# Attention pieces written between contraction steps, transposes two tiles behind scores, and the query-key products in one block

## The chip, the cores and the metric

One core of a Trainium2 chip. Its engines are TensorE (PE), VectorE (DVE), ScalarE (ACT), GpSimd (POOL) and SyncE (SP, which here issues most DMAs). The metric is the device time of one launch, in microseconds.

## What is computed

A decoder trunk of two layers over 512 tokens of width 1024. Layer 0 mixes tokens with a gated DeltaNet (6 heads of width 128), layer 1 with attention over a sliding window of 128 (12 heads of width 64, one sink logit per head). In both layers four heads also attend to 256 fixed memory tokens. Each layer ends in an output projection and a SwiGLU block. Cut to what the change touches:

```python
# layer 0: what the DeltaNet needs of its queries
qkv = silu(causal_depthwise_conv(proj, conv_w))            # q, k, v of six heads
intra = einsum("bhncd,bhnkd->bhnck", q, k) * decay          # query-key products
sol = triangular_solve(lower, rhs, unit_diagonal=True)      # then a scan over chunks
# both layers
def memory_attention(q, mem_k, mem_v):
    s = einsum("bshd,bmhd->bhsm", q, mem_k) * MEM_DH ** -0.5
    return einsum("bhsm,bmhd->bshd", softmax(s), mem_v)
# layer 1, per head; s is masked to the window
m = max(max(s), sink);  p = exp(s - m)
o = (p / (sum(p) + exp(sink - m))) @ v
x = x + concat([mix, mem_o]) @ w_out
```

## The kernel before

Activations lie transposed: eight tiles (k = 0 to 7) of 128 features by 512 tokens. A product with a weight (`project`) is a sum of eight contraction steps into one PSUM bank, and each step (`mm3`) is three matmuls of 128x512: high part of the weight by high and by low part of the activation, and low part of the weight by high part of the activation. The weight's high part `whi` is an ACT copy, its low part `wlo` a DVE subtraction; `split` makes an activation's pair `h`, `l` in the same way (copy L148, subtraction L161).

The code is written in program order, and a scheduler takes that order as priority when it places each engine's instructions. Each engine then works off its own queue in order, and semaphores hold an instruction until its inputs and its buffers are there. Named pools give the buffers; PSUM banks too come from pools (layer 0: three `pj`, two `g`, three `sc`; layer 1's attention: two `pj`, two `pt`, one each of `g`, `qk`, `sc`).

Attention for a tile of two heads is in four parts. `scores` makes the products of queries and keys (in `qk`, or in `g` and `sc` in layer 0) for the four blocks of 128 queries, and in layer 1 the masked row maxima (`sm`, `stats`). `soften` takes exponents and scales them by the reciprocal sums, half of the blocks on ACT (L148), half on DVE (L168). `weigh` transposes the probabilities on PE (L158, into `pt` or `g`), copies them out of PSUM (`pf`), multiplies with the values (into `sc`) and splits the result (`h`, `l`).

In layer 0 (`gdn`) the order is: scores of memory head pair 0, the inverse of the 32x32 diagonal blocks (`base_inverse`), query 0, transposes and sums of pair 0, query 1, scores of pair 1, query 2, transposes and sums of pair 1, and then a loop over the six heads, in which queries 3 to 5 are computed, each query tile gets its silu (ACT), and its product with the normalized keys `kn` goes to PE (bank `g`) and on to DVE. A query is a `project` and a depthwise convolution: one ACT copy with a scale and three DVE taps (`conv_tile`). The values' projection and the solve come next. The exponents need one table of ACT's functions, the silus another (`use`).

In layer 1 (`swa`) tiles 0 to 5 are window heads, 6 and 7 memory heads. For tile t the loop writes: the projection of the queries of tile t+1, scores of t, transposes and sums of t-1, the softmax of t. `output` then runs eight projections with w_out, one after the other.

Of the kernel before, what the change touches and what calls it, by code (L numbers as in the profile page):

```python
# [18 lines left out]
P = 128  # L19
T = 512  # L20
# [68 lines left out]
class Builder:  # L89
# [152 lines left out]
    def build(self):  # L242
        tc, nc, a = self.tc, self.nc, self.a
        with ExitStack() as st:
# [23 lines left out]
            with self.banks(pj=2, g=1, qk=1, pt=2, sc=1):  # L268
                with opened("swa", side="right") as sp:
                    mix = self.swa(sp)  # L270
                h = self.output(xp, 1, mix, self.apool)
# [185 lines left out]
    def normed(self, m):  # L457

        return self.project(self.a["win"][m], self.h)

    def conv_tile(self, m, out):

        ps = self.normed(m)
        tap = lambda j: self.gains[:, G_CONV + 4 * m + j:G_CONV + 4 * m + j + 1]
        self.copy(out, ps, scale=tap(3))
        for j in (2, 1, 0):
            s = 3 - j
            self.stt(out[:, s:], ps[:, :T - s], tap(j), out[:, s:], ALU.mult, ALU.add)
        return out

    def gdn(self, gp):
# [86 lines left out]
        query = lambda h: self.conv_tile(h, self.t(gp, [P, T], F32, "qv", 5))  # L558

        def remember(m):  # L560
            got = self.scores(gp, qm[m], self.memK[m], False)
            self.soften(gp, got, None)
            return got

        self.use(LN_EXP)
        got = remember(0)
        X, Tt = self.base_inverse(gp, base_in)
        for i in range(NH):
            h, c = divmod(i, NC)
            self.copy(kg[h][:, c, :], kg[h][:, c, :], scale=f[:, 2, i:i + 1])  # L570
        ts = [query(0)]
        self.weigh(gp, got, self.memV, 0, mq[0], False)
        ts.append(query(1))
        got = remember(1)
        ts.append(query(2))
        self.weigh(gp, got, self.memV, 1, mq[1], False)
        self.use(SILU_SIN)
        for h in range(H):
            if h + 3 < H:
                ts.append(query(h + 3))  # L580
            t = ts[h]
            self.fn(t, t, AF.Silu)
            ps = self.bank("g")
# [7 lines left out]
            nc.sync.dma_start(q2[h], sq)  # L591
        AT = DT
# [156 lines left out]
    def scores(self, pool, q, kk, win):  # L749

        nc = self.nc
        own = "pt" in self.pbufs
        half = [slice(0, 64), slice(64, P)]
        sm = [self.t(pool, [P, 2, 2, 2 * P], F32, "sm", 6 if own else 2) for _ in range(2)]
        sm = [t[:, n] for t in sm for n in range(2)]
        stats = self.t(pool, [P, 4, 2 * NC], F32, "stats", 3 if own else 2)
        mx, den, nm, es = (stats[:, i, :] for i in range(4))
        for n0 in range(0, NC, 2):
# [5 lines left out]
            for n in (n0, n0 + 1):  # L764
                ks = slice((n - 1) * P if n else 0, (n + 1) * P) if win else slice(0, ML)
                c0 = P if win and n == 0 else 0
                for b in range(2):
                    self.scored = self.mm(ps[b][:, n - n0, c0:], q[half[b], n * P:(n + 1) * P], kk[half[b], ks])
# [15 lines left out]
        return sm, mx, den, nm, es  # L784

    def soften(self, pool, scores, sinks):

        nc = self.nc
        win = sinks is not None
        sm, mx, den, nm, es = scores  # L790
        if win:
            sk = sinks.unsqueeze(2).to_broadcast([P, 2, NC])
            v4 = lambda ap: ap.rearrange("p (b n) -> p b n", b=2)
            self.stt(v4(mx), v4(mx), 0.125, sk, ALU.mult, ALU.max)
            self.ts(nm, mx, -1.0, ALU.mult)
            self.tt(nc.vector, v4(es), v4(nm), sk, ALU.add)
            self.fn(es, es, AF.Exp)
            for n in range(NC):
                c0 = 0 if n else P
                for b in range(2):  # L800
                    i = b * NC + n
                    self.fn(sm[n][:, b, c0:], sm[n][:, b, c0:], AF.Exp, scale=0.125, bias=nm[:, i:i + 1],
                            accum_out=den[:, i:i + 1])
            self.tt(nc.vector, den, den, es, ALU.add)
        nc.vector.reciprocal(den, den)
        for n in range(NC):
            k0 = 1 if win and n == 0 else 0
            p = sm[n][:, :, k0 * P:]
            dn = den.rearrange("p (b n) -> p n b", b=2)[:, n, :]
            for b in range(2):  # L810
                if n % 2:
                    self.copy(p[:, b], p[:, b], scale=dn[:, b:b + 1])
                else:
                    self.ts(p[:, b], p[:, b], dn[:, b:b + 1], ALU.mult)

    def weigh(self, pool, scores, vv, m, out, win):

        nc = self.nc
        own = "pt" in self.pbufs
        half = [slice(0, 64), slice(64, P)]  # L820
        sm = scores[0]
        o = self.bank("sc")
        group = NC if own else 2
        for n in range(NC):
            if n % group == 0:
                pf = {}
            k0 = 1 if win and n == 0 else 0
            pt = self.bank("pt" if own else "g", [P, 2, 2, P])
            for j in range(k0, 2):
                for b in range(2):  # L830
                    turned = self.tr(pt[:, j, b, :], sm[n][:, b, j * P:(j + 1) * P])
                    if own and self.scored is not None:

                        self.nosync(turned, self.scored)
                        self.scored = None
            pf[n] = self.t(pool, [P, 2, 2, P], F32, "pf", group)
            if own and n == 2:
                nc.vector.tensor_copy(pf[n][:, k0:], pt[:, k0:])
            else:
                self.copy(pf[n][:, k0:], pt[:, k0:])  # L840
            if (n + 1) % group:
                continue
            for n, t in pf.items():
                for j in range(1 if win and n == 0 else 0, 2):
                    for b in range(2):
                        v = vv[n - 1 + j][:, half[b]] if win else vv[j][:, m * P + 64 * b:m * P + 64 * b + 64]
                        ins = self.mm(o[half[b], n * P:(n + 1) * P], v, t[:, j, b, :], win and n == 0 or j == 0, j == 1)
                        if turned is not None:
                            self.nosync(ins, turned)
                            turned = None  # L850
        self.split(o, *out)


    def output(self, xp, layer, mix, hpool):
# [5 lines left out]
        for m in range(KD):  # L860
            ps = self.project(a["wout"][layer, m], mix, ("pj", "pj", "g")[m % 3],
                              (6, 7, 0, 1, 2, 3, 4, 5))
# [4 lines left out]
            self.acc = self.accumulate(xp, self.acc, self.x[m])  # L867
        return h
# [237 lines left out]
    def swa(self, sp):  # L1106
# [10 lines left out]
        def queries(t):  # L1117
            ps = self.project(a["wq"][t], h)
# [7 lines left out]
            else:  # L1126
                self.tt(nc.vector, qs[t], ps, self.rstd, ALU.mult)

        def keys():
            kk.append(self.t(sp, [P, T], F32, "ks"))  # L1130
            self.rope(sp, self.project(a["wkv"][0], hk), kk[0])

        def values():
            ps = self.project(a["wkv"][1], hk)
# [13 lines left out]
        def score(t):  # L1148
            got[t] = self.scores(sp, qs[t], kk[0] if t < 6 else memK[t - 6], t < 6)

        def soften(t):
            self.soften(sp, got[t], sinks[:, t, :] if t < 6 else None)

        def weigh(t):
            mix[t] = self.pair(self.bpool)
            if t < 6:
                self.weigh(sp, got[t], vv, t, mix[t], True)
            else:
                self.weigh(sp, got[t], memV, t - 6, mix[t], False)

        got = {}
        queries(6)
        queries(7)
        keys()
        values()
        score(6)
        soften(6)
        transpose_values()
        queries(0)
        score(7)  # L1170
        weigh(6)
        soften(7)
        last = 7
        for t in range(6):
            if t < 5:
                queries(t + 1)
            score(t)
            weigh(last)
            soften(t)
            last = t  # L1180
        weigh(last)
        return [mix[t] for t in range(KD)]
# [88 lines left out]
```

## Time and profile before

| What | Value |
|---|---|
| median of three runs | 1155.75 us |
| the three runs | 1155.51, 1155.75, 1159.62 us |
| the profiled execution | 1153.46 us, its span 1151.7 us |
| granted TensorE clock | 0.998 |
| PE busy | 1129.2 us, 98% of the span |
| DVE busy | 842.4 us, 73% |
| ACT busy | 632.1 us, 55% |
| POOL busy | 86.1 us, 7% |

A row of the timeline gives the start, the duration, the engine, the source line, the operation, what it writes and reads, the tile's shape, and how many instructions the row stands for; in brackets the engine's idle time before it and what ended that. Names lose their buffer numbers there. Start times are counted from the span's beginning.

### The profile page before, as it was taken

How to read it: one execution, taken by the hardware profiler on the slowest of the kernel's cores; microseconds unless marked ns; L12 is line 12 of the kernel's file. 1: busy time of each engine (PE TensorE's matmuls, PEld its weight loads, DVE VectorE, ACT ScalarE, POOL GpSimd, SP SyncE). 2: the span in 40 equal slices, each digit the busy share in tenths (PEclk: the TensorE clock that was granted, in tenths of full speed). 3: DMA queues.
4: the chain of work that ended last, by engine and by line, in shares of the span. 5: the costliest groups of instructions: out<-in, count | busy, mean ns of one | idle time of the engine just before them, and what ended most of it. 6: DMA issues, size and time to landing. Idle time of an engine off the chain costs nothing.

```text
span 1151.7 us, 19665 instructions
## 1 busy us (share of the span) xinstructions
PE 1129.2 (98%) x7476; PEld 990.3 (86%) x7476; DVE 842.4 (73%) x1587; ACT 632.1 (55%) x1271; POOL 86.1 (7%) x97
## 2 busy tenths in 40 slices
PE   7999999999999999999999999999999999999996
PEld 6888778887889998899998777778899988999986
DVE  5764877767789987389876767859799843898754
ACT  7579563366566652256654547675566622566533
POOL 0220000000111100011100000010011100111000
PEclk9999999999999999999999999999999999999999
DMA  8333342235557754567723421144478743577232
GB/s 310 118 121 110 120 101 95 85 106 162 167 138 186 191 126 127 160 147 187 181 69 103 134 79 38 40 110 129 115 186 193 180 112 103 147 190 184 70 95 93
DMA packets 73971, 152.83 MB, mean 133 GB/s; under 512 B 17756, under 2 KB 18420, under 8 KB 73876
## 3 DMA queue, kind: packets, MB, share of 16 engines
q1 hardware_dynamic: 62356, 130.59, 36.5%
q0 software_dynamic: 11520, 20.98, 11.6%
q8 instruction: 59, 0.97, 0.4%
q14 instruction: 36, 0.29, 0.1%
HBM read 144.58 MB, written 6.96 MB: 132 GB/s over the span
## 4 chain that ended last, share of the span: by engine, by line
PE 89%; DVE 6%; ACT 3%; DMA 1%; issue 1%; SPq 0%; DVEq 0%; ACTq 0%
PE pj L154 43%; PE g L154 38%; PE sc L154 5%; DVE wlo L161 2%; ACT sm L142 1%; PE pt L158 1%; PE qk L154 1%; ACT whi L148 1%; PE g L158 1%; DMA wraw<-in_wmk 1%; DVE stats L778 1%; DVE l L164 0%; DMA wraw<-in_win 0%; DVE x L164 0%; DVE btmp L161 0%
## 5 line engine op out<-in xcount | busy, mean ns | idle before, releaser
L148 ACT ACTIVATE whi<-wraw 128x512 fp32r<-128x512 f32 (+2 forms) x331 | 244.1, 746 | 253.6 <-PE pj L154 156.3
L161 DVE TENSOR_TENSOR wlo<-wraw,whi 128x512 fp32r<-128x512 f32 (+2 forms) x331 | 274.5, 839 | 104.7 <-ACT whi L148 98.4
L154 PE MATMUL pj<-h,whi 128*128 128x512 f32 (+1 forms) x676 | 266.4, 396 | 0.0
L154 PE MATMUL pj<-l,whi 128*128 128x512 f32 (+1 forms) x676 | 264.7, 392 | 0.4 <-DVE l L164 0.4
L154 PE MATMUL pj<-h,wlo 128*128 128x512 f32 (+1 forms) x676 | 264.0, 391 | 0.0
L154 PE MATMUL g<-T,whi 128*128 128x256 f32 x1280 | 228.1, 278 | 0.2
L154 PEld LDWEIGHTS g<-T,whi 128*128 128x128 f32 x1280 | 194.7, 188 | 1.8 <-DVE fu L164 1.8
L154 PE MATMUL g<-T,wlo 128*128 128x256 f32 x640 | 177.8, 278 | 0.0
L154 PEld LDWEIGHTS pj<-h,whi 128*128 128x128 f32 x676 | 126.8, 188 | 29.4 <-issue 3.6
L154 PEld LDWEIGHTS pj<-l,whi 128*128 128x128 f32 x676 | 127.1, 188 | 27.3 <-issue 1.8
L154 PEld LDWEIGHTS pj<-h,wlo 128*128 128x128 f32 x676 | 127.0, 188 | 25.7 <-issue 0.8
L154 PE MATMUL g<-l,whi 128*128 128x256 f32 (+1 forms) x508 | 144.4, 284 | 0.0
L154 PE MATMUL g<-h,whi 128*128 128x256 f32 (+1 forms) x508 | 144.3, 284 | 0.0
L154 PE MATMUL g<-h,wlo 128*128 128x256 f32 (+1 forms) x508 | 144.3, 284 | 0.0
L154 PEld LDWEIGHTS g<-T,wlo 128*128 128x128 f32 x640 | 120.1, 188 | 0.0
L154 PEld LDWEIGHTS g<-l,whi 128*128 128x128 f32 x508 | 95.3, 188 | 1.4 <-issue 0.2
L154 PEld LDWEIGHTS g<-h,whi 128*128 128x128 f32 x508 | 95.3, 188 | 1.2
L154 PEld LDWEIGHTS g<-h,wlo 128*128 128x128 f32 x508 | 95.3, 188 | 1.0
L1014 POOL DMA_DIRECT2D ws<-in_wgu x40 | 35.1, 877 | 707.9 <-DMA ws<-in_wgu 255.1
L148 ACT ACTIVATE whi<-ws 128x512 fp32r<-128x512 f32 x80 | 50.4, 630 | 49.0 <-PE g L154 40.2
L161 DVE TENSOR_TENSOR fu<-pj,rstd 128x512 f32<-128x512 f32 (+1 forms) x34 | 22.4, 660 | 54.2 <-PE pj L154 54.2
L161 DVE TENSOR_TENSOR wlo<-ws,whi 128x512 fp32r<-128x512 f32 x80 | 54.9, 686 | 6.4 <-ACT whi L148 6.3
(345 smaller groups left out, 1620.7 us busy)
## 6 DMA issues: line engine op xcount, KB each, us to landing
wraw<-in_wgu SPq DMA_DIRECT2D x48, 512.0 KB, 4.3
ws<-in_wgu SPq DMA_DIRECT2D x80, 256.0 KB, 3.5
ws<-in_wgu POOLq DMA_DIRECT2D x80, 256.0 KB, 4.7
wraw<-in_wdn SPq DMA_DIRECT2D x48, 384.0 KB, 3.1
wraw<-in_win SPq DMA_DIRECT2D x26, 512.0 KB, 3.6
wraw<-in_wgu SPq DMA_DIRECT2D x40, 256.0 KB, 4.5
wraw<-in_wout SPq DMA_DIRECT2D x16, 512.0 KB, 3.6
wraw<-in_wdn SPq DMA_DIRECT2D x16, 256.0 KB, 2.7
```

Of the source, the lines that this page charges most:

```text
L142: ins = self.nc.scalar.activation(out, in_, func, **kw).ins
L148: self.copied = self.nc.scalar.activation(out, in_, AF.Copy, **kw).ins
L154: return self.nc.tensor.matmul(out, lhsT, rhs, start=start, stop=stop, skip_group_check=more).ins
L158: return self.nc.tensor.transpose(out, in_, self.ident[:k, :k]).ins
L161: return eng.tensor_tensor(out=out, in0=a, in1=b, op=op).ins
L778: nc.vector.tensor_reduce(out=mx[:, i:i + 2], in_=ps[b], op=ALU.max, axis=AX.X)
L1014: nc.gpsimd.dma_start(s1, a22, accum_op=ALU.add)
```

## The change

The functions `scores`, `soften` and `weigh` become one, `attend`, which computes nothing when it is called but returns the pieces of a tile's attention as callables: `score0`, `score1` (two blocks of queries each), `soften`, `turn0`, `turn1` (transposes and their copies), `sum0`, `sum1`. `project` takes a table `between` that says after which contraction step which pieces are written.

```diff
-    def project(self, src, acts, tag="pj", order=range(KD), w=None):
+    def project(self, src, acts, tag="pj", order=range(KD), w=None, between=None):
         w = self.weight(src) if w is None else w
         ps = self.bank(tag)
         for n, k in enumerate(order):
             self.mm3(ps, w, k, acts[k], n == 0, n == KD - 1)
+            for step in (between or {}).get(n, ()):
+                step()
         return ps
```

Layer 0. The pieces of pair 0 go into query 1, those of pair 1 into queries 2, 4 and 5. All six queries come first, then all silus, each ordered behind the last copy of turned probabilities (`self.turned`), and the six products in one block. The sixth query uses the buffer `big`.

```diff
-        ts = [query(0)]
-        self.weigh(gp, got, self.memV, 0, mq[0], False)
-        ts.append(query(1))
-        got = remember(1)
-        ts.append(query(2))
-        self.weigh(gp, got, self.memV, 1, mq[1], False)
-        self.use(SILU_SIN)
-        for h in range(H):
-            if h + 3 < H:
-                ts.append(query(h + 3))
...
+        query(0)
+        query(1, {5: [att[0]["turn0"]], 7: [att[0]["sum0"], att[0]["turn1"]]})
+        query(2, {1: [att[0]["sum1"], att[1]["score0"], att[1]["score1"], att[1]["soften"]]})
+        query(3)
+        query(4, {2: [att[1]["turn0"]], 5: [att[1]["sum0"], att[1]["turn1"]]})
+        query(5, {0: [att[1]["sum1"]]})
+        self.use(SILU_SIN)
+        for h in range(H):
+            self.nosync(self.fn(ts[h], ts[h], AF.Silu), self.turned)
+            against(h, "sc" if h % 2 else "g")
```

Layer 1. Transposes and sums of a window tile come two tiles after its scores, and its softmax one projection later than its scores. The last three tiles' pieces go between the steps of the output's rows 0 to 2 (`rest`), whose sums are now held open in three banks; `output` therefore runs inside the pool of `swa`.

```diff
+        queries(2, {4: step(0, "soften") + step(1, "score0"), 7: step(1, "score1")})
+        for t in range(2, 5):
+            queries(t + 1, {5: step(t - 2, "turn0") + step(t, "score0"),
+                            7: step(t - 2, "turn1") + step(t - 1, "soften") + step(t, "score1") + step(t - 2, "sum0", "sum1")})
...
+        def rest(row):
+            do = lambda t, *names: [f() for f in step(t, *names)]
+            row(0, 6, 7, 0)
+            do(3, "turn0"), do(5, "score0")
+            row(0, 1, 2)
+            do(3, "turn1"), do(4, "soften"), do(5, "score1"), do(3, "sum0", "sum1")
+            row(1, 6, 7, 0)
+            do(4, "turn0")
+            row(1, 1, 2)
+            do(4, "turn1")
+            do(5, "soften")
+            row(0, 3)
+            row(1, 3)
+            do(4, "sum0", "sum1")
...
+            row(2, 3, 4, 5)
```

In `output` a helper `row(m, *ks)` adds the steps `ks` to the sum of row m and finishes the row when all eight are in.

What this does to the order of the instructions, at three places. In the rows, a name's number tells one buffer from another and differs between the two kernels.

PE in layer 0 around the first memory pair, before: `pj_1457` is query 0, `pj_1540` query 1, `g_` the transposes, `sc_1486` the sum.

```order
L154 MATMUL pj_1457<-h_489,wlo_1454 128x512
L158 MATMUL g_1487<-consts_66,sm_1272 128x128 x4
L158 MATMUL g_1494<-consts_66,sm_1272 128x128 x4
L154 MATMUL pj_1540<-h_454,whi_1536 128x512
L154 MATMUL pj_1540<-l_455,whi_1536 128x512
L154 MATMUL sc_1486<-pf_1492,mv_53_295 64x128 x2
L154 MATMUL sc_1486<-pf_1492,mv_55_322 64x128 x2
```

And now, where `pj_1493` is query 1:

```order
L154 MATMUL pj_1493<-h_479,wlo_1490 128x512
L158 MATMUL g_1512<-consts_66,sm_1273 128x128 x4
L158 MATMUL g_1519<-consts_66,sm_1273 128x128 x4
L154 MATMUL pj_1493<-h_484,whi_1489 128x512
L154 MATMUL pj_1493<-l_485,whi_1489 128x512
L154 MATMUL pj_1493<-h_484,wlo_1490 128x512
L154 MATMUL pj_1493<-h_489,whi_1489 128x512
L154 MATMUL pj_1493<-l_490,whi_1489 128x512
L154 MATMUL pj_1493<-h_489,wlo_1490 128x512
L154 MATMUL sc_1532<-pf_1517,mv_53_295 64x128 x2
L154 MATMUL sc_1532<-pf_1517,mv_55_322 64x128 x2
```

The transposes moved from the end of query 0 to a place eighteen matmuls into query 1, and six matmuls instead of two stand between them and the sum.

ACT in layer 1, one window tile, before: `stats_7450` is the sinks' exponent, `sm_7448` and `sm_7449` the exponents and then their scalings, `whi_7960` a weight's copy, `h_7469` the split of the tile before.

```order
L142 ACTIVATE sm_7448,stats_7450<-sm_7448,stats_7450 128x128
L142 ACTIVATE stats_7450<-stats_7450 128x8
L142 ACTIVATE sm_7448,stats_7450<-sm_7448,stats_7450 128x128
L142 ACTIVATE sm_7448,stats_7450<-sm_7448,stats_7450 128x256
L148 ACTIVATE h_7469<-sc_7471 128x512
L142 ACTIVATE sm_7448,stats_7450<-sm_7448,stats_7450 128x256
L142 ACTIVATE sm_7449,stats_7450<-sm_7449,stats_7450 128x256 x4
L148 ACTIVATE whi_7960<-wraw_7958 128x1024
L148 ACTIVATE sm_7448<-sm_7448,stats_7450 128x256 x2
L148 ACTIVATE sm_7449<-sm_7449,stats_7450 128x256 x2
L148 ACTIVATE pf_7600<-pt_7597 128x256
L148 ACTIVATE pf_7607<-pt_7602 128x512
```

And now (`stats_7387`; `h_7266` is the split of the tile two before):

```order
L142 ACTIVATE stats_7387<-stats_7387 128x8
L142 ACTIVATE sm_7388,stats_7387<-sm_7388,stats_7387 128x128
L142 ACTIVATE sm_7388,stats_7387<-sm_7388,stats_7387 128x256
L148 ACTIVATE pf_7503<-pt_7500 128x256
L148 ACTIVATE pf_7510<-pt_7505 128x512
L142 ACTIVATE sm_7388,stats_7387<-sm_7388,stats_7387 128x256
L142 ACTIVATE sm_7440,stats_7387<-sm_7440,stats_7387 128x256 x4
L148 ACTIVATE whi_7835<-wraw_7833 128x1024
L148 ACTIVATE pf_7541<-pt_7536 128x512
L148 ACTIVATE sm_7388<-sm_7388,stats_7387 128x256 x2
L148 ACTIVATE sm_7440<-sm_7440,stats_7387 128x256 x2
L148 ACTIVATE h_7266<-sc_7575 128x512
```

The copies of turned probabilities moved in among the exponents and behind the weight's copy, and the split from among the exponents to behind the scalings.

DVE in the same tile, before: the maxima's scaling, two small rows that the sinks' exponent needs, and the split's subtraction `l_7470`, with the weight's `wlo_7923` ahead of the four rows of maxima (L774).

```order
L161 TENSOR_TENSOR wlo_7923<-wraw_7920,whi_7922 128x1024
...
L838 COPY pf_7489<-pt_7484 128x512
L164 SCALAR_TENSOR_TENSOR stats_7450<-stats_7450,small_68 128x8
L168 TENSOR_SCALAR stats_7450<-stats_7450 128x8
L161 TENSOR_TENSOR stats_7450<-stats_7450,small_68 128x8
L161 TENSOR_TENSOR l_7470<-sc_7471,h_7469 128x512
```

And now:

```order
L161 TENSOR_TENSOR l_7151<-sc_7450,h_7150 128x512
L161 TENSOR_TENSOR q_7467<-q_7467,rs_7468 128x512
L164 SCALAR_TENSOR_TENSOR stats_7387<-stats_7387,small_68 128x8
L161 TENSOR_TENSOR wlo_7728<-wraw_7725,whi_7727 128x1024
L168 TENSOR_SCALAR stats_7387<-stats_7387 128x8
L161 TENSOR_TENSOR stats_7387<-stats_7387,small_68 128x8
```

The two small rows moved behind the split's subtraction, the rotated queries `q` and the weight's low part.

More of the change, by code (lines that the diff above doesn't have):

```diff
@@ L746, in scan_step, with attend, score @@
         return new
-    def scores(self, pool, q, kk, win):
+    def attend(self, pool, q, kk, vv, m, out, sinks):
         nc = self.nc
+        win = sinks is not None
         own = "pt" in self.pbufs
         half = [slice(0, 64), slice(64, P)]
[L754 to L758, printed above, removed]
+        s = {}
+        sm, pf = [None] * NC, [None] * NC
+        def score(n0):
+            if n0 == 0:
+                s["stats"] = self.t(pool, [P, 4, 2 * NC], F32, "stats", 3 if own else 2)
+            tile = self.t(pool, [P, 2, 2, 2 * P], F32, "sm", 6 if own else 2)
+            sm[n0:n0 + 2] = [tile[:, n] for n in range(2)]
+            mx, den, nm, es = (s["stats"][:, i, :] for i in range(4))
             if own:
@@ L805, in soften @@
[L805 to L812, printed above, removed]
-                else:
[L814 to L843, printed above, removed]
@@ L846, in weigh, with output @@
                         v = vv[n - 1 + j][:, half[b]] if win else vv[j][:, m * P + 64 * b:m * P + 64 * b + 64]
[L847 to L854, printed above, removed]
+                        self.mm(o[half[b], n * P:(n + 1) * P], v, pf[n][:, j, b, :], win and n == 0 or j == 0, j == 1)
+            if n0:
+                self.split(o, *out)
+        return {"soften": soften} | {f"{name}{i}": (lambda f=f, i=i: f(2 * i))
+                                     for name, f in (("score", score), ("turn", turn), ("sum", weigh)) for i in range(2)}
+    def output(self, xp, layer, mix, hpool, ahead=None):
         nc, a = self.nc, self.a
@@ L859, in output, with row @@
         self.acc = None
[L860 to L862 removed]
+        rows = {}
+        def row(m, *ks):
+            if m not in rows:
+                rows[m] = self.weight(a["wout"][layer, m]), self.bank(("pj", "pj", "g")[m % 3]), []
+            w, ps, done = rows[m]
+            for k in ks:
+                self.mm3(ps, w, k, mix[k], not done, len(done) == KD - 1)
+                done.append(k)
+            if len(done) < KD:
+                return
             self.tt(nc.vector, self.x[m], ps, self.x[m], ALU.add)
@@ L867, in output @@
             self.acc = self.accumulate(xp, self.acc, self.x[m])
+        if ahead is not None:
+            ahead(row)
+        for m in range(len(h), KD):
+            row(m, 6, 7, 0, 1, 2, 3, 4, 5)
         return h
@@ L1146, in transpose_values @@
             vv.extend(vt[:, c, :] for c in range(NC))
[L1148 to L1161, printed above, removed]
+        att = {}
@@ L1162, in swa @@
+        step = lambda t, *names: [att[t][n] for n in names]
         queries(6)
         queries(7)
[L1164 to L1182, printed above, removed]
+        keys({0: step(6, "score0"), 5: step(6, "score1")})
@@ L1184, in final @@
+        return [mix[t] for t in range(KD)], rest
     def final(self, fp, squares, t):
```

128 lines of the change are left out of this document (85 added, 43 removed).

## The prediction

> **What bounds the kernel now.** I read the table of windows first, cut at the places where the kernel changes its work: layer 0's queries and memory attention (129.6 to 185.3), its solve and scan (to 283.3), and layer 1's attention (672.9 to 773.5). Behind each window's length stand the busy times of PE, PE's weight loads, DVE, ACT and POOL, then PE's clock, the DMA share and GB/s.
>
> ```profile
> 129.60:185.30 55.70, 52.22 (x361) 41.99 (x360) 44.67 (x99) 33.32 (x72) 0.00 (x0) 1.00 0.32 87
> 185.30:283.30 98.00, 97.63 (x754) 78.16 (x753) 69.10 (x140) 47.70 (x100) 0.00 (x0) 1.00 0.32 101
> 672.90:773.50 100.60, 98.99 (x698) 74.57 (x698) 70.48 (x233) 70.33 (x210) 2.60 (x3) 1.00 0.20 60
> ```
>
> PE sets the end in all three: it is idle 3.48 us in the first, 0.37 in the second, 1.61 in the third, at full clock. So a change of order can bring back only PE's waits and its cost of switching between kinds of matmul. The waits by releaser say which of them belong to attention:
>
> ```profile
> PE g L158 <- DVE sm L168: 2.9, 2, 1.9
> PE pt L158 <- DVE sm L168: 0.5, 1, 0.5
> PE sc L154 <- ACT pf L148: 0.5, 1, 0.5
> PE qk L154 <- ACT sm L142: 0.5, 1, 0.5
> PE pt L158 <- ACT pf L148: 0.3, 1, 0.3
> ```
>
> Two of them (2.9, two stalls, and 0.5 on pf) lie in layer 0's memory attention, three (1.3) in layer 1. Here are layer 0's on PE's timeline:
>
> ```profile
> 136.69 0.39 PE L154 MATMUL pj<-l,whi 128*128 128x512 f32 x1
> 136.92 0.39 PE L154 MATMUL pj<-h,wlo 128*128 128x512 f32 x1
> 138.26 1.15 PE L158 MATMUL g<-consts,sm 128*128 128x128 f32 x8 [0.95 <-DVE sm L168]
> 139.48 0.40 PE L154 MATMUL pj<-l,whi 128*128 128x512 f32 x1
> 140.41 1.14 PE L154 MATMUL sc<-pf,mv 128*64 128x128 f32 x16 [0.53 <-ACT pf L148]
> 142.33 0.47 PE L154 MATMUL pj<-h,wlo 128*128 128x512 f32 x1
> 142.88 1.15 PE L154 MATMUL sc<-pf,mv 128*64 128x128 f32 x16
> 159.23 0.39 PE L154 MATMUL pj<-h,whi 128*128 128x512 f32 x1
> 161.54 0.83 PE L158 MATMUL g<-consts,sm 128*128 128x128 f32 x5 [1.92 <-DVE sm L168]
> 163.46 0.40 PE L154 MATMUL pj<-h,wlo 128*128 128x512 f32 x1
> 163.79 1.09 PE L154 MATMUL sc<-pf,mv 128*64 128x128 f32 x16
> ```
>
> Two steps of a projection start 0.23 apart (136.69, 136.92) though each lasts 0.39, so a wait costs the distance of the starts less 0.23: 1.11 before 138.26, 0.70 before 140.41, 0.32 before 142.88, 2.08 before 161.54, together 4.21. An insertion that waits for nothing (163.46 to 163.79, 0.33) costs 0.10 going in, and about as much coming out. Without these 0.10s, the four waits are 3.8 us. [...]
>
> **The change, layer 0.** What PE waited for there is the end of a softmax:
>
> ```profile
> 156.85 2.12 ACT L148 ACTIVATE big<-big 96x1024 f32<-96x1024 f32 x1 [0.19 <-DVE big L161]
> 161.04 1.14 DVE L168 TENSOR_SCALAR sm<-sm,stats 128x256 f32<-128x256 f32 x4
> 161.24 1.70 ACT L148 ACTIVATE sm<-sm,stats 128x256 f32<-128x256 f32 x4
> 163.92 1.28 ACT L133 ACT_TABLE_LOAD   x1
> 181.10 1.95 PE L154 MATMUL g<-qv,kn 128*128 128x128 f32 x16
> 181.30 0.69 ACT L148 ACTIVATE qv<-pj,gains 128x512 f32<-128x512 f32 x1 [2.13 <-PE pj L154]
> 185.37 0.63 ACT L142 ACTIVATE qv<-qv 128x512 f32<-128x512 f32 x1 [1.92 <-DVE qv L164]
> ```
>
> 1. First memory head. Its scaled scores were ready at about 138.2 (first pair) and 139.2. The transposes now stand after step 5 of query 1, and query 0 ends at about 137.2 (5.44 of steps, and the inverse's small matmuls between); 18 steps of 0.23 later is 141.3: nothing to wait for. The sum stands 6 steps later (143.7), with pf copied by 142.9. Second head: its scores come in query 2 instead of on the far side of the inverse's own steps, its transposes in query 4 at 162.6; the four copies that scale it end at about 161.4 to 162 by the rows of 161.04 and 161.24 (ACT does the 2.12 us copy of `big` ahead of them, as before). About 0.6 to 1 us of slack; if that cover were gone, the price is what it was, 2.08. Taken: all 3.8 us of waits go.
>
> 2. Insertions. Two or three fewer in this stretch: the query-key products stood in five places and stand in two, the second head's transposes in two and stand in one; the solve is split in one place more. 3 x 0.2 = 0.6 gained. The products themselves cost the same (1.95 for 16 records, which is two heads).
>
> 3. Products in one block. They now need all silus first. PE reaches them at 175.8; the last silu needs query 5's tile (PE done at 175.7), its copy, three DVE taps and its own time. Before, that took from PE's end (181.1) through the copy (181.30) to the end of the silu (186.0) 4.9 us, so about 180.6 to 180.9. The sixth product follows five others (5 x 0.94) and five steps of the values' projection (1.1), at 181.7. Cover about 1 us: if DVE is later than I count, PE waits by that amount. What is late next: the solve's first part now has the steps of the values' projection in other places, two fewer used by its second part (2 x 0.23); I take 0.5 as loss (bounds 0 and 1.1, the five steps that are used up earlier).
>
> 4. Nothing: the silu table load (1.28) is moved ahead of ACT's copy of `big`, which then ends near 159.8 instead of 158.97, inside the slack of step 1 (uncovered it costs PE 0.8); query 5 written into `big`; one issue on SP's queue moved by one place, none on POOL's. From the values' projection on, PE's order is as before, and the scan's window has PE idle 0.37 of 98, so an earlier start is kept.
>
> Sum of layer 0: -3.8 - 0.6 + 0.5 = -3.9 us. Bounds: -4.5 (no loss in the solve) and -1.0 (the second head's 2.08 and about 1 at the last product come back).
>
> **The change, layer 1.** One window tile of before on PE, and ACT's and DVE's rows for it:
>
> ```profile
> 718.20 0.93 PE L154 MATMUL qk<-ks,q 64*128 64x128 f32 x8
> 723.18 1.13 PE L154 MATMUL qk<-ks,q 64*128 64x256 f32 x8
> 724.24 1.57 PE L158 MATMUL pt<-consts,sm 128*128 128x128 f32 x10
> 725.89 0.60 PE L158 MATMUL pt<-consts,sm 128*128 128x128 f32 x4
> 726.42 1.75 PE L154 MATMUL sc<-pf,vt 128*64 128x128 f32 x28
> ...
> 724.72 1.04 ACT L148 ACTIVATE pf<-pt 128x256 f32<-128x256 f32 x2 [2.24 <-PE pt L158]
> 727.40 0.20 ACT L142 ACTIVATE stats<-stats 128x8 f32<-128x8 f32 x1
> 728.38 0.58 ACT L148 ACTIVATE h<-sc 128x512 fp32r<-128x512 f32 x1
> 731.32 1.05 ACT L148 ACTIVATE whi<-wraw 128x1024 fp32r<-128x1024 f32 x1
> 732.27 1.69 ACT L148 ACTIVATE sm<-sm,stats 128x256 f32<-128x256 f32 x4
> 739.07 0.19 ACT L142 ACTIVATE stats<-stats 128x8 f32<-128x8 f32 x1
> ...
> 728.99 0.69 DVE L161 TENSOR_TENSOR l<-sc,h 128x512 fp32r<-128x512 f32 x1 [1.96 <-ACT h L148]
> 732.01 0.64 DVE L161 TENSOR_TENSOR q<-q,rs 128x512 f32<-128x512 f32 x1
> 734.38 1.22 DVE L161 TENSOR_TENSOR wlo<-wraw,whi 128x1024 fp32r<-128x1024 f32 x1
> ```
>
> The sinks' exponent (stats, L142) returns every 11.67 us (727.40 to 739.07); that is a tile. PE fills it: 24 steps 5.44, scores 1.9, fourteen transposes 1.5, sum 1.7, three insertions 0.6, waits 0.5.
>
> 5. PE alone: one insertion fewer per tile and no wait for softmax: 11.0. Were PE the only limit, four full tiles would give 4 x 0.65 = 2.6 us.
>
> 6. The new loop. In the changed order ACT does, from one sinks' exponent: the eight exponents (3.4: from 727.40 to 731.32 less `h`, which is no longer among them) with two pf copies between (0.9, by the 1.04 of 724.72), whi (0.95), the third pf (0.5), four scalings (1.6), and only then `h` of the tile two before (0.5): about 8.2 us. DVE has `l` behind `h` (0.7), `q` (0.55), the maximum's scaling, wlo (1.2), and two 128x8 rows (about 0.2 each, as the one at 727.40) on which the next sinks' exponent waits. With hand-overs that is an estimate of 11.3 to 11.4 us. So the tile would be set by ACT and DVE's queues in turn, near what it was: 11.35 for 11.67, four times, -1.3. The Trainium skill, "Perfetto Trace Analysis", section "Tensor Engine Instruction (MATMUL, LD_WEIGHTS)", has ACT and DVE as strictly first in, first out; the trace agrees in that `h` ran among the exponents (728.38), where its queue has it, and no run here shows one overtaken. By that rule the loop counts whole; without it, step 5's 2.6 would hold.
>
> 7. Start and end. These are estimates. In tile 1 the sum waits for a pf copy that stands behind the exponents and whi (5.8 after the sinks' exponent by step 6, PE is there at about 5): 0.85. Scores of tile 2 wait for a `q` behind wlo, half of its 1.22: 0.65. In the last tiles the transposes have two banks, each free after its copy (half of 724.72's 1.04, once): 0.6; and the output's row 0 waits for the split of tile 4, half of `l`: 0.35. That is 2.4, of which before's waits at such places (0.5 + 0.5 + 0.3) cover 1.3, so +1.1 to +1.3. The output rows 0 to 2 have the same steps as before.
>
> Sum of layer 1: -1.3 + 1.2 = -0.1. Bounds: -3.9 (step 5 and before's 1.3 of waits, nothing new) and +2.4 (no tile shorter, all new waits).
>
> Together -4.0. The profiled execution took 1153.46 (span 1151.7), 2.3 below the median of 1155.75, which is outside the three runs; -4.0 taken off the median is 1151.8, and off the profiled one 1149.5.
>
> **Rivals.**
> - Both parts gain. If the loop is shorter than I count by 0.35 us (its hand-overs are an estimate), PE's 11.0 sets the tile: 1155.75 - 3.9 - 2.6 = 1149.3. For it: ACT is busy 70.33 of 100.6, DVE 70.48, so neither is full. Against: step 6 is a latency and not a load.
> - Slower: the loop is longer than a tile was. It decides from 12.7 us per tile, where four tiles lose 4 x 1.0 and the layer-0 gain is gone: one wait of ACT for PE inside it (2.24 stands at 724.72 today, for transposes) would do. With 13.0: 4 x 1.35 + 1.2 - 3.9 = +2.7, 1158.4. Against: the transposes there now come two tiles late and their inputs are long done.
> - It doesn't do what it says in layer 0: the second head's transposes again wait, and the last product too, -1.0 in place of -3.9, with layer 1 unchanged: 1154.7. For it: slacks of 0.6 to 1 us. Against: the first head's slack is 2.
>
> **How the numbers follow.** About 0.5% (5.8 us) is what can be told from no change here. My forecast 1151.8 has 0.47, both parts gain 0.26, layer 0 fails 0.15, slower 0.12. The case at 1149.3 passes the bound of 1149.97 in four of five, and the forecast, with its own spread of 1149.5 to 1154, seldom: faster 0.24. Slower than 1161.5 needs a tile of 13.8 us: 0.04. The rest, 0.72, is the same. The range goes from 1147.8 (a little inside both lower bounds together, 1147.4) to 1156.5 and leaves out the slower case's upper half and a tail below.
>
> **What would show it.** Right: no mark of PE waiting for sm or pf in the first window, the first 64-wide solve about 4 us earlier against the start, and a distance between sinks' exponents near 11.35 with `l`, `q` and wlo gapless between `h` and the next. Wrong: distances near 11.0 (step 6 doesn't bind), or above 12, with a new wait on ACT ahead of a pf copy; a wait of PE for qv or big at the sixth product (step 3); or PE's idle time in the scan's window grown by what layer 0 saved (step 4).

## The result, and the profile after

| | before | changed |
|---|---|---|
| median | 1155.63 us (6 runs, 1154.29 to 1159.62) | 1148.32 us (6 runs, 1147.96 to 1148.94) |
| profiled execution | 1153.46, span 1151.7 | 1148.39, span 1146.6 |

The ratio is 0.9936, 95% interval 0.9922 to 0.9949: 0.64% faster. The medians are 7.3 us apart, the two profiled executions 5.1. That these differ is a part of the answer: the profile of before was taken from an execution that was shorter than all six of its runs in this comparison.

The windows of both kernels are cut at the same pieces of work: from the first scores of layer 0 to its output, from there to the first projection of layer 1, from there to row 3 of layer 1's output, and from there to the end. Behind each length stand the busy times of PE, its weight loads, DVE, ACT and POOL, then PE's clock, the DMA share and GB/s. Before:

```profile
129.60:283.30 153.70, 149.84 (x1113) 120.14 (x1113) 113.77 (x238) 81.03 (x172) 0.00 (x0) 1.00 0.32 96
283.30:655.60 372.30, 371.85 (x2451) 340.32 (x2450) 294.52 (x496) 196.43 (x340) 34.82 (x40) 1.00 0.57 149
655.60:773.50 117.90, 116.29 (x772) 88.27 (x771) 80.36 (x247) 74.81 (x215) 2.60 (x3) 1.00 0.23 70
773.50:1151.70 378.20, 369.20 (x2495) 340.18 (x2493) 274.93 (x467) 189.39 (x339) 34.60 (x39) 0.99 0.54 139
```

Changed:

```profile
129.30:279.60 150.30, 149.40 (x1114) 120.38 (x1114) 112.91 (x238) 80.57 (x172) 0.00 (x0) 1.00 0.33 98
279.60:651.90 372.30, 371.85 (x2452) 340.31 (x2451) 294.66 (x496) 196.28 (x340) 34.79 (x40) 1.00 0.57 149
651.90:768.40 116.50, 115.04 (x771) 88.94 (x770) 79.97 (x248) 74.76 (x215) 3.45 (x4) 1.00 0.26 74
768.40:1146.60 378.20, 369.25 (x2495) 340.32 (x2493) 274.74 (x466) 189.44 (x338) 33.66 (x38) 0.99 0.53 138
```

Layer 0 is 3.4 us shorter, layer 1's attention 1.4, and the two blocks between and behind them are equal to the tenth. The other 0.3 lies ahead of the first window. The two gains are not of one kind. In layer 0 PE's idle time (length less busy) falls from 3.86 to 0.90 us, which is most of the gain. In layer 1 it falls only from 1.61 to 1.46; there it is the busy time that falls, from 116.29 to 115.04.

Layer 0 on PE's timeline, changed (the rows that answer to the four waits of before, some of the block of products, and two rows of the scan and behind it):

```profile
140.70 0.39 PE L154 MATMUL pj<-h,wlo 128*128 128x512 f32 x1
140.94 1.03 PE L158 MATMUL g<-consts,sm 128*128 128x128 f32 x8
143.30 1.09 PE L154 MATMUL sc<-pf,mv 128*64 128x128 f32 x16
161.39 1.03 PE L158 MATMUL g<-consts,sm 128*128 128x128 f32 x8
164.50 1.14 PE L154 MATMUL sc<-pf,mv 128*64 128x128 f32 x16
174.60 1.05 PE L154 MATMUL g<-qv,kn 128*128 128x128 f32 x8
178.17 1.06 PE L154 MATMUL g<-qv,kn 128*128 128x128 f32 x8
180.23 1.05 PE L154 MATMUL sc<-big,kn 128*128 128x128 f32 x8
251.69 0.49 PE L154 MATMUL sc<-S,kn 128*128 128x128 f32 x2 [0.28 <-ACT gcr L148]
266.11 1.98 PE L154 MATMUL g<-N,consts 128*128 128x512 f32 x4 [0.62 <-DVE N L161]
```

No attention row has a wait any more in this profile, and the products stand side by side. The row at 251.69 is one of the scan, and in before it is this:

```profile
255.98 0.49 PE L154 MATMUL sc<-S,kn 128*128 128x128 f32 x2 [0.28 <-ACT gcr L148]
```

Counted from the first scores (129.61 in before, 129.31 now) that is 126.4 and 122.4, so 4.0 us are saved up to there. At 266.11 some 0.6 of it is given back. DVE's row behind that shows what was waited for:

```profile
265.37 2.00 DVE L161 TENSOR_TENSOR N<-N,kn 128x512 f32<-128x512 f32 x3 [3.00 <-DMA kn<-q]
```

N waits for a transfer: the squared queries, which layer 0 had put to DRAM, come back into the buffer of the keys, which is free only after the scan's last use of them. The profile of before has no such wait at this place, but another profile of it does (b2, below).

In layer 1 the waits of PE and one period of ACT and DVE:

```profile
PE qk L154 <- DVE q L161: 0.4, 1, 0.4
PE sc L154 <- ACT pf L148: 0.3, 1, 0.3
PE pt L158 <- ACT pf L148: 0.2, 1, 0.2
PE pj L154 <- ACT h L148: 0.2, 1, 0.2
PE pj L154 <- DVE l L161: 0.2, 1, 0.2
...
720.52 0.19 ACT L142 ACTIVATE stats<-stats 128x8 f32<-128x8 f32 x1
724.70 1.05 ACT L148 ACTIVATE whi<-wraw 128x1024 fp32r<-128x1024 f32 x1
727.72 0.58 ACT L148 ACTIVATE h<-sc 128x512 fp32r<-128x512 f32 x1
731.49 0.19 ACT L142 ACTIVATE stats<-stats 128x8 f32<-128x8 f32 x1
...
728.48 0.69 DVE L161 TENSOR_TENSOR l<-sc,h 128x512 fp32r<-128x512 f32 x1
729.08 0.68 DVE L161 TENSOR_TENSOR q<-q,rs 128x512 f32<-128x512 f32 x1
729.76 1.22 DVE L161 TENSOR_TENSOR wlo<-wraw,whi 128x1024 fp32r<-128x1024 f32 x1
731.09 0.17 DVE L161 TENSOR_TENSOR stats<-stats,small 128x8 f32<-128x8 f32 x1
```

The loop through the two queues is there as drawn, `h`, `l`, `q`, wlo, small rows, next sinks' exponent, without a gap. It takes 10.97 us from exponent to exponent, not 11.35. The new waits of PE add up to 1.3 us, as much as the three of before there (0.5, 0.5 and 0.3). So layer 1's gain does not come from waits; PE goes from the wide matmuls to small ones and back 25 times in that window instead of 27, and what each of these changes saves was not measured.

### The profile page after: what moved, and what is told of

Its sections match the earlier page's. It is cut to its first block, busy times and chain, and to the rows that moved or that the text cites. A ratio compares the mean times of both kernels' runs of the same rounds, so it can differ in the third digit from the quotient of the medians.

```text
span 1146.6 us, 19668 instructions
## 1 busy us (share of the span) xinstructions
PE 1127.0 (98%) x7476; PEld 990.7 (86%) x7476; DVE 841.2 (73%) x1587; ACT 631.5 (55%) x1271; POOL 86.0 (7%) x97
## 4 chain that ended last, share of the span: by engine, by line
PE 89%; DVE 5%; ACT 4%; DMA 1%; issue 1%; SPq 0%; DVEq 0%; ACTq 0%
PE pj L154 44%; PE g L154 38%; PE sc L154 6%; ACT sm L142 2%; DVE wlo L161 1%; PE g L158 1%; DMA wraw<-in_wmk 1%; DVE q L161 0%; DVE sm L784 0%; PE qk L154 0%; ACT sm L148 0%; DVE l L164 0%; ACT whi L148 0%; ACT pf L148 0%; DVE l L161 0%
```

## The experiments

Times below are medians, and each ratio is to the kernel before, executed beside it on the same chip. From each profile I also take two distances between rows on PE: from layer 0's first scores to the last row ahead of layer 1's first projection ("layer 0", with its SwiGLU block, which is constant), and from there to the end ("layer 1", with its block).

| kernel | layer 0 | layer 1 |
|---|---|---|
| before | 526.0 | 496.1 |
| changed | 522.6 | 494.7 |

**Each layer alone.** e1 takes `gdn`, `project` and `attend` from the change and layer 1 from before; e2 the reverse.

```text
e1   gdn, project, normed, conv_tile, attend   as changed
     swa, output                               as before
e2   gdn                                       as before
     swa, output, attend                       as changed
```

> Layer 0 as changed, layer 1 as before. Theory (the waits of PE are the gain, each layer's by itself): the profiles show 4.0 us saved from the first scores to the scan and 0.5 given back at the end of the scan, so 3.5 to 4.0 us less than before, about 1152. Rival one (before's longer runs lose their time in layer 0, where PE waited): about 6 less, near 1149.5, with runs within 1 us of each other. Rival two (layer 0's saving shows only together with layer 1's): within 1.5 us of before.

> Layer 1 as changed, layer 0 as before. Theory: 1.3 us less than before, as between the two profiles, about 1154.3. Rival one: before's longer runs lose their time in layer 1, so about 3.5 less, near 1152, with runs close together. Rival two (the new order of ACT and DVE costs what PE saves): no difference.

e1: 1150.58, ratio 0.9964 (0.995 to 0.9978), layer 0 522.5, layer 1 497.5. e2: 1152.54, ratio 0.9981 (0.9972 to 0.999), layer 0 526.0, layer 1 494.8. So each layer gains by itself, 3.9 and 1.9 us against the 1154.45 of before there, and neither needs the other. The 3.9 is what was expected of layer 0; the 1.9 lies between the 1.3 of the theory and the 3.5 of the rival, nearer to the theory. Together they are 5.8, and the change took off 6.7 to 7.6 in its three comparisons; the intervals of the ratios are wide enough for this difference. Layer 1 of e1 is before's, and 1.4 us longer than in before's first profile: before scatters there.

**The pieces without the block.** e3 leaves the pieces between the steps, and puts silus and products back into a loop with the queries, without the silus' place behind the copies.

```diff
+        late = {3: None, 4: {2: [att[1]["turn0"]], 5: [att[1]["sum0"], att[1]["turn1"]]}, 5: {0: [att[1]["sum1"]]}}
         for h in range(H):
-            self.nosync(self.fn(ts[h], ts[h], AF.Silu), self.turned)
-            against(h, "sc" if h % 2 else "g")
+            if h + 3 < H:
+                query(h + 3, late[h + 3])
+            self.fn(ts[h], ts[h], AF.Silu)
+            against(h, "g")
```

> The change, but with layer 0's silus and query-key products in a loop with the queries, as before, and without the silus' place behind the copies; the attention pieces stay between the steps. Theory (waits are the gain, the block saves three or four switches at 0.2): 0.6 to 0.8 us longer than the change, about 1149. Rival (the block is a main part of the gain, because silus ahead of the pf copies make PE wait for pf again): 2 us or more longer than the change, 1150.5 or above, with marks of PE waiting for pf.

e3: 1150.93, ratio 0.9967 (0.9953 to 0.998); layer 1 494.7, layer 0 526.3, no shorter than before in this profile. The time is the rival's, though not by its cause: in layer 0 PE doesn't wait for pf, but for the first silu. Here are PE and ACT of e3, and the two windows in which its clock was low (the clock, as a share of full speed, is the third number from the right):

```profile
158.69 0.39 PE L154 MATMUL pj<-h,wlo 128*128 128x512 f32 x1
162.02 1.16 PE L154 MATMUL g<-qv,kn 128*128 128x128 f32 x8 [2.95 <-ACT qv L142]
163.60 0.63 PE L154 MATMUL pj<-h,wlo 128*128 128x512 f32 x1
164.03 0.63 PE L154 MATMUL pj<-h,whi 128*128 128x512 f32 x1
...
155.89 1.28 ACT L133 ACT_TABLE_LOAD   x1
157.19 2.10 ACT L148 ACTIVATE big<-big 96x1024 f32<-96x1024 f32 x1
159.19 1.69 ACT L148 ACTIVATE sm<-sm,stats 128x256 f32<-128x256 f32 x4
161.35 1.14 ACT L142 ACTIVATE qv<-qv 128x512 f32<-128x512 f32 x2
...
162.50:165.00 2.50, 2.50 (x13) 2.07 (x12) 2.50 (x5) 2.50 (x4) 0.00 (x0) 0.67 1.06 158
165.00:167.50 2.50, 2.50 (x14) 2.01 (x12) 2.50 (x4) 1.20 (x3) 0.00 (x0) 0.65 1.27 188
```

The silu stands behind the second head's exponents, the table load, the copy of `big` and the scalings. Before, the product came after that head's transposes and sums, which had done the waiting; with those moved two queries on, the product waits in their place (162.02 - 158.69 - 0.23 = 3.1 us). And then the steps run 0.43 apart instead of 0.23: the granted clock was 0.67 and 0.65 in these two windows of 2.5 us, so 0.8 and 0.9 us of clock were lost, 1.7 together. In this profile the wait costs a second time.

Without that 1.7, e3's layer 0 would be 1.4 us shorter than before's. The times say the same. e2 and e3 ran on one chip and differ in layer 0 alone, and e3 is 1.6 shorter (1150.93 against 1152.54). So the pieces alone do save something in layer 0, about 1.5 us of the 3.5 to 3.8.

**The block without the pieces.** e8 keeps the six queries first and the block, and writes the attention whole between the queries, where it stood.

```diff
+        do = lambda m, *names: [att[m][n]() for n in names]
         query(0)
...
+        do(0, "turn0", "sum0", "turn1", "sum1")
+        query(1)
+        do(1, "score0", "score1", "soften")
+        query(2)
+        do(1, "turn0", "sum0", "turn1", "sum1")
         query(3)
...
+        query(4)
+        query(5)
```

> The change, but in layer 0 the attention pieces stand whole between the queries, where they were before; silus and products stay in one block behind all six queries. Theory (pieces between the steps take PE's four waits away, the block gives those steps the silus' cover, and neither does much alone): PE's waits of 0.95, 0.5 and 1.9 come back, layer 0 is within 1 us of before, and the whole 2.5 to 3.5 us longer than the change. Rival (the block alone is the gain in layer 0): within 1 us of the change.

e8: 1153.24, ratio 0.9976 (0.9965 to 0.9986), 5.3 longer than the change beside it (1147.97); layer 0 526.4, layer 1 494.7. The waits are back, as expected:

```profile
PE g L158 <- DVE sm L168: 3.0, 2, 1.9
PE sc L154 <- ACT pf L148: 0.8, 2, 0.5
```

In profiles the difference to the change is 4.1 (spans 1150.0 and 1145.9), more than the 2.5 to 3.5 I expected, and all in layer 0. So the block alone saves nothing in layer 0 that can be seen: +0.4 against before in its profile, and by the times e8 is 2.3 shorter than its before, where e2, which has layer 1's change alone, is 1.9 shorter. The pieces alone save about 1.5, both together 3.5 to 3.8. The changes between kinds of matmul that I counted as a gain of the block by itself don't show.

**What sets the tile in layer 1.** e5 gives ACT 0.5 us more in each window tile, among the exponents; e6 makes eight transposes of each tile twice.

```diff
 # e5
+                    if n == 2:
+                        self.copy(self.t(pool, [P, 2 * P], F32, "idle"), sm[n][:, 0, :])
...
 # e6
-                        self.tr(pt[:, j, b, :], sm[n][:, b, j * P:(j + 1) * P])
+                        for _ in range(2 if win and n > 1 else 1):
+                            self.tr(pt[:, j, b, :], sm[n][:, b, j * P:(j + 1) * P])
```

> The change itself, once more, as the measure for the three others. By the first comparison 6 to 7.5 us less than before; if the first comparison's before was on its long side by chance, 5 to 6.

> The change with a copy of 128x256 on ACT (0.5 us) more among the exponents of each window tile; nothing reads it. Theory (PE sets the tile in layer 1, ACT and DVE follow): under 0.7 us longer than the change. Rival (the loop through ACT's and DVE's queues, gapless at 10.97 us in the profile of the change, sets it): 0.5 in each of four to five tiles, 2.0 to 2.5 us longer, and sinks' exponents 11.4 apart.

> The change with eight transposes of each window tile made twice (into the same place). Theory (PE sets the tile): 8 x 0.12 in six tiles, 5 to 6 us longer than the change. Rival (the loop sets it): PE has room, under 2 us longer, most of it in the last two tiles.

The change beside them: 1147.97, ratio 0.9933 (0.9918 to 0.9947). e6: 1152.76, ratio 0.9976 (0.9966 to 0.9985), 4.8 longer, a little under the 5 to 6 expected; its layer 1 takes 499.2 for 494.7, and the last sum of the attention comes 4.57 later: 0.76 of each tile's 0.96 reaches the end. So PE sets the tile. e5: 1149.87, ratio 0.9952 (0.9935 to 0.9969), 1.9 longer, which is between the two forecasts. In the middle tiles its sinks' exponents are 11.28 apart instead of 10.97 (one distance, ahead of these two rows, is shorter, 9.93):

```profile
720.10 0.19 ACT L142 ACTIVATE stats<-stats 128x8 f32<-128x8 f32 x1
731.38 0.19 ACT L142 ACTIVATE stats<-stats 128x8 f32<-128x8 f32 x1
```

But the attention's last sum is only 0.53 later, for 3 us of ACT; the other 0.7 of the 1.2 by which layer 1 is longer (495.9) comes behind it, with a weight that landed late (next experiment). So the loop exists and stretches by 0.31 for 0.49 put in, but little of it reaches PE in six tiles. PE is the bound, and the loop comes next, close behind. The runs of e5 scatter from 1148.2 to 1153.0, and its longest were not profiled.

**Where before's scatter lies.** Two more profiles of the kernel before.

> The kernel before, for another profile. Its runs lie from 1152.4 to 1159.6 us, those of the change within 1.5. Theory (in before the fourth weight of layer 1's output is asked for just behind a burst of weights for the next block, and lands 5.5 to 7.3 us later, by chance): layer 0 and layer 1's attention as in the first profile to 0.3 us (526.0 and 117.8), and a longer run shows its excess between the output's row 3 and the first step of the next block, with a late landing. Rival: the excess lies in the waits of layer 0 or is spread over all windows.

> As the run ahead of it: one more profile of the kernel before, for the place of its scatter.

They took 1159.44 and 1154.63. b3: layer 0 526.1, layer 1 497.7. b2: layer 0 528.4, layer 1 500.0. The attention of layer 1 is the same in all: its last sum begins 111.4 to 111.5 behind the window's start in before, b2, b3 and e1. What differs is, first, a weight of the output. By its place in the order it is the sixth of eight, not the fourth as I had it. ACT's row that waits for it, in before:

```profile
779.16 1.06 ACT L148 ACTIVATE whi<-wraw 128x1024 fp32r<-128x1024 f32 x1 [2.83 <-DMA wraw<-in_wout]
```

The same in e1, which has the same layer 1, and PE's row at the start of the next block there:

```profile
777.03 1.06 ACT L148 ACTIVATE whi<-wraw 128x1024 fp32r<-128x1024 f32 x1 [4.61 <-DMA wraw<-in_wout]
803.07 0.50 PE L154 MATMUL pj<-l,whi 128*128 128x512 f32 x1 [0.88 <-DVE l L164]
```

And in the changed kernel:

```profile
773.03 1.06 ACT L148 ACTIVATE whi<-wraw 128x1024 fp32r<-128x1024 f32 x1 [1.96 <-DMA wraw<-in_wout]
```

This transfer took from issue to landing 5.5, 7.3, 7.2 and 7.3 us in the four profiles with before's layer 1 (before, b2, b3, e1), and 4.0 to 4.8 in the eight with the changed one and nothing added. At 7.2 or more PE waited 0.9 to 1.6 us for the split activations of the next block, at 5.5 or less never (e5: 6.5, and a wait of 0.3). The change moves that request away from others: before, POOL's last request for the next block's weights goes out at 773.56 and the output's at 773.60; now at 766.25 and 768.42. The two are at most 0.1 us apart in all four profiles with before's layer 1, and 2.2 to 2.7 apart in the eight with the changed one.

Second, b2 shows PE at half its clock behind two of its waits. Its wait for the scaled probabilities is as long as in the first profile of before; then:

```profile
161.38 0.83 PE L158 MATMUL g<-consts,sm 128*128 128x128 f32 x5 [1.92 <-DVE sm L168]
163.07 0.63 PE L154 MATMUL pj<-h,whi 128*128 128x512 f32 x1
163.50 0.63 PE L154 MATMUL pj<-l,whi 128*128 128x512 f32 x1
...
162.50:165.00 2.50, 2.50 (x13) 1.66 (x13) 1.68 (x3) 2.48 (x4) 0.00 (x0) 0.52 1.04 158
165.00:167.50 2.50, 2.50 (x24) 2.28 (x21) 0.69 (x1) 1.20 (x4) 0.00 (x0) 0.80 0.62 76
805.00:810.00 5.00, 3.39 (x14) 2.30 (x13) 5.00 (x9) 3.35 (x5) 0.00 (x0) 1.00 0.24 88
810.00:815.00 5.00, 5.00 (x14) 3.31 (x14) 4.58 (x9) 3.09 (x5) 0.00 (x0) 0.66 0.31 103
```

Steps are 0.43 apart while the clock is low, which loses 1.2 and 0.5 us by the clocks of 0.52 and 0.80, 1.7 together; the row of the scan shown above comes 128.1 behind the first scores instead of 126.4. The same happens again behind the late weight (810 to 815, clock 0.66, 1.7 us). Layer 0 of b2 has one more thing, the wait of N for the fetched squares, and PE waits 0.7 us for it:

```profile
271.12 1.93 DVE L161 TENSOR_TENSOR N<-N,kn 128x512 f32<-128x512 f32 x3 [3.08 <-DMA kn<-q]
```

So the 2.4 us by which its layer 0 is longer are the clock's 1.7 and this 0.7. Of the theory, the place behind row 3 holds for b3; in b2 the rival holds as well, since 2.4 of its 5.9 are in layer 0.

How often the half clock comes in runs that were not profiled can be read roughly from their mean granted clock, which is on record for each. One such loss of 1.7 us lowers the mean over 1152 us by 0.0015. (The last 6 to 9 us of every profile are at half clock too, and this difference moves the mean by up to 0.0013, so the count is not exact.) Of the 51 executions of before beside the experiments, 23 have 0.996 or less, with a median of 1155.94; the other 28 have a median of 1154.09. Of the 17 executions of the change none is below 0.997.

**The fetch that gave 0.6 back.** e7 and e9 are one kernel: the squared queries come back into a query tile's buffer.

```diff
-                t = self.t(gp, [P, T], F32, f"kn{h}")
+                t = self.t(gp, [P, T], F32, "qv", 5)
                 nc.sync.dma_start(t, q2[h])
```

> The change, with the squared queries fetched back at the end of layer 0's scan into a buffer that is free earlier (a query tile's instead of the keys'). Theory (the fetch ends last there, 3.0 us of DVE's wait in the profile of the change, and PE waits 0.6 for it): 0.5 to 0.8 us shorter than the change, about 1147.6, and no wait of PE for N. Rival (another input of N comes as late): within 0.2 us of the change.

> The change a third time, as the measure for the early fetch beside it: 1148 us.

> The change with the early fetch of the squared queries, beside the change on the same chip. Theory: the fetch's landing varies (3.5 to 4 us), PE waited for it in one profile of the change (0.6) and not in the other, so 0.2 to 0.6 us shorter than the change in the median and runs a little closer together. Rival: nothing that can be told from zero, since the saving is taken back at the output's first steps.

e7: 1147.51, ratio 0.9937 (0.9924 to 0.9951). Beside each other, the change took 1148.26 (1146.99 to 1149.19, ratio 0.9943, 0.9931 to 0.9956) and e9 1147.55 (1147.22 to 1147.99, ratio 0.9937, 0.9923 to 0.995). The mark of PE waiting for N (0.6 and 0.8) is in two of six profiles of the changed layer 0, in none of the two with the early fetch, and in one of six with before's layer 0 or a part of it (b2, 0.7). So this wait comes and goes by chance, and it is not shown that the change brought it. With five runs of each, 0.7 apart in the median and with ranges that overlap, the gain is not told from zero by the times, and two profiles without a wait that four of six others lack too settle little. Its medians are the lowest seen.

## Why the prediction was right or wrong

The time lies in the range, 0.5 us inside its lower end, and the sign is right, but not by the likeliest case: -4.0 was forecast, -5.1 came between the profiles and -7.3 between the medians. The first rival, both layers gain, with 1149.3, was the nearest, and e6 shows its mechanism: PE sets the tile. Its number is partly luck, since it leaves out step 7's +1.2 and knows nothing of the scatter below.

- Steps 1 to 3 (layer 0, -3.9): right in the sum. Transposes came at 140.94 and 161.39 (forecast 141.3 and 162.6), the sixth product at 180.23 (181.7) without a wait, 4.0 us were saved up to the scan. The slack that I gave as 0.6 to 1 us is thin: the sum of the second pair waited for pf in six of eight profiles of the changed layer 0, from 0.25 to 0.65 us (0.65 in e1, 0.56 in the change's third profile).
- What the sum had wrong was that its terms could be added. I let the waits (-3.8) and the block (-0.6 + 0.5) stand apart. e3 and e8 show that they belong together: the pieces alone save about 1.5 in place of 3.8, since a wait of 3.1 comes back at the first product unless the products are last, and the block alone saves nothing that can be seen.
- Step 4, an earlier start is kept: it failed by 0.6 in the profile of the change, by the transfer into the keys' buffer, and held in others. b2 has the same wait without the change. I went by PE's idle time in one profile and left the transfers behind the scan out.
- Step 6: mis-sized. I put the loop at 11.35 us and it took 10.97, so it stayed beside PE's tile instead of above it, which is the first of the prediction's own signs of being wrong. The piece that was too long is ACT's: `h` began 7.2 behind the sinks' exponent (720.52 to 727.72), and I had 7.7. It was a slip of adding: the terms of step 6 (3.4, 0.9, 0.95, 0.5, 1.6 and 0.5) make 7.85 and not 8.2. The 0.35 between the two is just what the first rival asked for. The Trainium skill, "Perfetto Trace Analysis", section "Tensor Engine Instruction (MATMUL, LD_WEIGHTS)", calls ACT and DVE strictly first in, first out. The trace agrees: ACT's and DVE's rows of this period stand in the order of their queues.
- Steps 5 and 7: of 2.4 us of new waits 1.3 are there (0.4, 0.3 and three of 0.2), mostly at the places named, and they cancel the 1.3 of before. PE's two middle tiles took 11.0 and 11.5 (step 5 had 11.0), so layer 1 gains 1.4, neither 0.1 nor 2.6.
- The working had no term for what lies outside PE's order: the profile of before was a short execution (1153.46 of runs from 1152.4 to 1159.6). In the profiles the change also takes away two chances of losing time, the late weight of the output and the half clock behind a wait. An estimate from the numbers above: 3.5 for layer 0, 1.4 for layer 1, 1.0 for the half clock (the median of before's 51 executions, 1155.05, less the 1154.09), and 1.1 for the late weight (1.4 to 1.6 us longer in e1 and b3, and seen in three of four profiles) make 7.0, where the three comparisons gave 6.7 to 7.6. How often the weight is late in runs without a profile stays open.

## What to carry to other kernels

When a stall is taken away, look for the next instruction on that engine whose input comes from the same queue: here most of the wait would have moved to the products, and the two parts of the edit are worth more than twice as much together as their single gains added up. Read more than one profile where the runs of a kernel differ by more than the gain looked for; the one at hand may hide what a change is really worth, as it did for the kernel before and for e3. A wait of two microseconds on PE can cost nearly twice its length, as in b2 (2.1 us, and then 1.7 of clock).

## What the runs showed of the hardware

A wait of PE of about 2.1 us (1.92 marked idle) was followed by half clock in one of five profiles that have it, one of 3.1 us in the one that has it, and two waits of 0.74 and 0.87 close together once; steps went from 0.23 to 0.43 us apart, and each time the granted clock was 0.50 for 3.4 us (162.6 to 166.0 and 811.1 to 814.5 in b2, 163.3 to 166.7 in e3), from 1.2 to 1.4 us after the wait had ended. The Trainium skill, "TensorE: Matmul & The Clock Gate", section "What's actually happening", gives about 3.4 us of idle as what brings the slow clock, by a window that runs freely. The half clock and its chance character agree with the trace; the length doesn't: here less than 3.4 us of idle was enough, and the measurement decides.

Going from 128x512 steps to small matmuls cost 0.10 us more than a step where nothing waited and the small ones were sums (163.46 to 163.79 in before), and 0.01 where they were transposes (140.70 to 140.94 in the change), so it is not one price. The sixth weight of layer 1's output, 512 KB, landed 5.5 to 7.3 us after its issue where it was asked for within 0.1 us of POOL's last request, and 4.0 to 4.8 where 2.2 to 2.7 us lay between. That the neighbours in the queues decide it is read from the issue times and was not tested by an experiment of its own.
